# Adding the experts' rows to the residual by accumulating DMAs at the ends of two layers of a one-core kernel

## The chip, the cores and the metric

The kernel runs on one core of a Trainium2 chip, as one launch. The metric is the device time of a run in microseconds (us); of several runs the median is taken.

## The reference

Two layers of a hybrid block over 512 tokens of 1024 values and 256 context tokens. What matters here is the second part of each layer, a mixture of experts, and the step behind it:

```python
hl2 = rmsnorm(xl, g_ffn[l]) * (1 + sc2) + sh2
y = hierarchical_moe(...)          # each token: 2 of 32 experts, (silu(x@w1[e]) * (x@w3[e])) @ w2[e], weighted
xl = xl + ga2 * y                  # the residual; in layer 0 the context rows too
...
return rmsnorm(xl, g_final)        # after layer 1
```

The next layer begins with another `rmsnorm` of the residual, so nothing of it can start on a token tile before that tile's sum is complete. All data are float32.

## The kernel before

The residual lies in SBUF as one tile `X` of 128 partitions x `nt` token tiles x 1024 values, with `nt` = 6 in layer 0 (four token tiles and two of context) and 4 in layer 1. It is filled before the experts start and not touched while they run.

The experts run in the order `seq`, one after another. Their weights come from HBM as six 1 MB pieces each (`eparts`), through a ring of SBUF buffers (`wcycle`, counted by `wcount`), issued by SP in the order of use. An expert gathers its rows (`gather`, an indirect DMA from POOL), multiplies by w1 and w3 (`first`), goes through the activation (`mid`, `hidden`), multiplies by w2 (`second`) and weighs its rows (`out`). The rows of 30 of the 32 experts are then scattered by an indirect DMA from POOL (`send`, line 1528) into a DRAM tensor `yd[l]`, which has two places, `c` = 0 and 1, for each token. The last two experts share a `Group` whose rows stay in SBUF as a high and a low part (`split`); they reach the tokens as a product with a one-hot matrix.

At the end of a layer the loop takes `nt` more buffers from the ring, and SP reads both places of each token tile back, 1 MB a tile (`backs`, line 2010). These reads stand in SP's queue behind the last expert's weights, and wait for the last `send`. VectorE adds them to `X`, two additions a tile (line 2133). The last expert's `second` has two halves of 512 columns; their PSUM is the two banks of one tile `self.p`, the second half reusing the bank that `first` had filled. `end(hf)` evacuates a half (copy `hc` on ScalarE, sum `hs` on VectorE, weight `wg` on VectorE, then the split `keep`). `combine(n_, hf)` forms, for the n_-th tile of `order`, the product with the one-hot matrix plus `ident` x `X` in PSUM, and ScalarE copies the result to `X` (line 2120). From tile n_ = 2 on its PSUM is the tile `acc` (one buffer, `pacc`) or `po` by turns. When both halves of a tile are there, `inv_rms` squares it on ScalarE and POOL makes the two steps to the inverse root (lines 413 and 414). In layer 1 `final` scales and stores the tile; its factor `gfin` is read by a DMA of 512 KB that SP issues ahead of the last expert's six weight pieces, into a buffer taken outside the ring's turn.

A scheduler orders each engine's instructions by its own estimate of when they are ready, unless edges are drawn: `ordered("V", YORD[l])` draws them on VectorE through the additions and the steps of `end`. `SEQ` is the order of the combines on TensorE, in layer 1

```python
((0, 0), "l", (1, 0), (2, 0), (3, 0), (0, 1), (1, 1), (2, 1), (3, 1), 0, 1, 2, 3)
```

where "l" is the second half's `keep` and a bare number is a `final`.

Of the kernel before, what the change touches and what calls it, by code (L numbers as in the profile page):

```python
# [13 lines left out]
ALU = mybir.AluOpType  # L14
# [4 lines left out]
D = 1024  # L19
# [4 lines left out]
NE = 32  # L24
# [17 lines left out]
def xs(n_):  # L42
# [68 lines left out]
DIAG = (1, 1)  # L111
SCT = (1, 1)
LATE = (2, 2)
YORD = ([("hT",), ("y", 0, 0), ("y", 0, 1), ("y", 1, 0), ("hs", 0), ("wg", 0), ("y", 1, 1), ("keep", 1, 0),
# [3 lines left out]
YLB = (3, 3)  # L118
WPRE = (4, 3)
WPS = ("ss", "sa")  # L120
# [135 lines left out]
def program(tc, a, out, dbg=None):  # L256
# [23 lines left out]
    V, S, G, T = [Chained(e_) for e_ in (nc.vector, nc.scalar, nc.gpsimd, nc.tensor)]  # L280
    Y = nc.sync
# [11 lines left out]
    yd = [dr.tile([2 * n_, D], F32, name=f"yd{l}") for l, n_ in enumerate((NT, NL))]  # L293
# [20 lines left out]
    def pacc():  # L314
        return ps.tile([128, 512], F32, name="acc", bufs=1)
# [33 lines left out]
    def wtile(pool=None, n=6, dt=F32):  # L349
        return (pool or wt).tile([128, 2048], dt, name="w", bufs=n)  # L350
# [65 lines left out]
    mark = {}  # L416
# [18 lines left out]
    ct = lambda c_, x_, y_: x_ if c_ else y_  # L435
# [9 lines left out]
    X = xp_.tile([128, 6, D], F32, name="X")  # L445
# [10 lines left out]
    for l in range(2):  # L456
        last = l == 1
# [524 lines left out]
        def wsplit(hf):  # L982

            if hf:
                raw = dfp.tile([128, 4, NT], F32, name="ks1").rearrange("p g t -> p (g t)").rearrange("p (k f) -> p k f", f=512)
                raws = [raw[:, 0:4], raw[:, 4:6]]
            else:
                raws = [wtile().rearrange("p (k f) -> p k f", f=512) for _ in range(2)]
            for w, k0, n in ((raws[0], 0, 4), (raws[1], 4, 2)):
                Y.dma_start(w[:, 0:n], w_out[:, k0:k0 + n, 512 * hf:512 * hf + 512])  # L990
            yield 1
            u = [wtile(dt=F32R).rearrange("p (k f) -> p k f", f=512) for _ in range(3)]
            for i in range(3):
                w, h, lo_ = raws[i // 2][:, 2 * (i % 2):2 * (i % 2) + 2], u[i // 2][:, 2 * (i % 2):2 * (i % 2) + 2], u[(i + 3) // 2][:, 2 * ((i + 1) % 2):2 * ((i + 1) % 2) + 2]
                split(h, lo_, w, V if i in WSV[l] else G)
                if hf:
                    yield 1
            yield [(u[k // 4][:, k % 4], u[(k + 6) // 4][:, (k + 2) % 4]) for k in range(6)]

        wg = [wsplit(0), wsplit(1)]  # L1000
# [10 lines left out]
        X = xp_.tile([128, nt, D], F32, name="X")  # L1011
# [4 lines left out]
        nw2 = NW2[l] - NWA[l]  # L1016
        wta = P.open(f"wta{l}")
        wcount, held = [0], [None]
        wcycle = [(lambda: wta, NWA[l])] * NWA[l] + [(lambda: wt2, nw2)] * nw2 + [(lambda: wt3, 4)] * 4
# [6 lines left out]
        def eparts(e, eng=Y, tail=False):  # L1026
            for nm in ("w1", "w3", "w2"):
                src = wsource(nm, e)
                n = src.shape[1] // 2
                cut = tail and nm == "w2"  # L1030
                for h in range(2):
                    pl, nb = wcycle[wcount[0] % len(wcycle)]
                    w = wtile(pl() if callable(pl) else pl, nb)
                    wcount[0] += 1
                    held[0] = (Y if wcount[0] > SPIN[l] else eng).dma_start(w.rearrange("p (k f) -> p k f", k=2 * n if cut else n),
                                                               src[:, :, 512 * h:512 * h + 512] if cut else src[:, n * h:n * h + n, :])
                    yield w
# [311 lines left out]
        wt2 = P.open(f"wt2{l}")  # L1349
# [139 lines left out]
        wts = pins  # L1489
# [33 lines left out]
        def column(s):  # L1523
            return idn[:, place(s), :]
# [94 lines left out]
        class Expert:  # L1619
# [79 lines left out]
            def second(self):  # L1699

                hT, w2 = self.hT, self.w2
                if self.tail:
                    for hf in range(2):
                        py = self.p[:, ct(hf, slice(0, 512), slice(512, 1024))]
                        for k in range(0, 4, 2):
                            for g in range(2):
                                o = 64 * hf + 32 * g
                                T.matmul(py[o:o + 32, :], hT[:, k + g, 0:32], w2(k + g, hf), start=(k == 0), stop=(k == 2))  # L1708
                            yield 1
                elif self.cap == 32:  # L1710
                    py = self.p[:, 512:1024]
                    for k in range(0, 4, 2):
                        for g in range(4):
                            T.matmul(py[32 * g:32 * g + 32, :], hT[:, k + g // 2, 0:32], w2(k + g // 2, g % 2), start=(k == 0), stop=(k == 2))  # L1714
                        yield 1
                elif self.cap == 64:
                    py = self.p[:, 512:1024]
                    for k in range(4):
                        T.matmul(py[0:64, :], hT[:, k, 0:64], w2(k, 0), start=(k == 0), stop=(k == 3))  # L1719
                        T.matmul(py[64:128, :], hT[:, k, 0:64], w2(k, 1), start=(k == 0), stop=(k == 3))  # L1720
                        yield 1
                else:
                    for hf in range(2):
                        for k in range(4):
                            T.matmul(self.p[:, 512 * hf:512 * hf + 512], hT[:, k, :], w2(k, hf), start=(k == 0), stop=(k == 3))  # L1725
                            yield 1
# [37 lines left out]

            def end(self, hf):

                r, py, g = self.r, self.p[:, ct(hf, slice(0, 512), slice(512, 1024))], self.g
                yl, ys = g.tiles(True)
                sl = slice(512 * hf, 512 * hf + 512)
                h_ = self.hs[32 * hf:32 * hf + 32]  # L1770
                mark["S", "hc", hf] = S.copy(h_, py[64 * hf:64 * hf + 32])
                mark["V", "hs", hf] = V.tensor_tensor(ys[r, sl], py[64 * hf + 32:64 * hf + 64], h_, op=ALU.add)
                mark["V", "wg", hf] = g.weigh(r, hf, sl, ys[r, sl], self.weights())
                yield 1
                g.split(r, hf, yl[64 + r.start:64 + r.stop, sl], 1)
# [58 lines left out]
        def load(n_):  # L1834
            s = seq[n_]
            if s not in wts:
                v = nc.values_load(sid[0:1, s:s + 1], engines=[mybir.EngineType.SP], min_val=0, max_val=NE - 1,
                                   skip_runtime_bounds_check_because=why)
                if last and n_ == NE - 1:
                    gfin.append(wtile(wt2, nw2)[:, 0:D])  # L1840
                    Y.dma_start(gfin[0], a["g_final"].to_broadcast([128, D]))
                wts[s] = list(eparts(v, tail=n_ == NE - 1))

        def gather(n_, idxt, o):
            G.indirect_dma_start(out=o[0:n_, :], out_offset=None, in_=h2d[l][0:nrow, :],  # L1845
# [142 lines left out]
                        pass  # L1988
            ovp.release()

        gfin, es, early, backs = [], [], [], {}
        for n_ in range(NE + 1):
            f = None
            if n_ < NE:
                s = seq[n_]
# [3 lines left out]
                else:  # L1999
                    g = Group(column(s), slots[:, place(s):place(s) + 1] if SCT[l] and n_ < NE - LATE[l] else None)  # L2000
                    small_[0] = g if capacity(l, s) == 32 else None
                f = make(n_, g)
                es.append(f)
                g.apart = APT[l] and n_ >= NE - 2
            if n_ == NE - 1 and SCT[l]:
                for t in ct(last, (0, 1, 2, 3), (4, 5, 0, 1, 2, 3)):
                    pl, nb = wcycle[wcount[0] % len(wcycle)]
                    backs[t] = wtile(pl() if callable(pl) else pl, nb).rearrange("p (c f) -> p c f", c=2)
                    wcount[0] += 1
                    Y.dma_start(backs[t], yd[l].rearrange("(c t p) d -> t p c d", c=2, p=128)[t])  # L2010
            if n_ == NE - 1:
                mark.clear()
                if not last:
# [21 lines left out]
            nb = {32: 2, 64: 4, 128: 8}[e.cap]  # L2035
# [36 lines left out]
            c = run(e.steps, max(0, na - e.done - TUR[l]))  # L2072
# [33 lines left out]
        g = es[-1].g  # L2106
# [23 lines left out]

        for n_, t in enumerate(order) if SCT[l] else ():
            for c_ in range(2):
                mark["V", "y", n_, c_] = V.tensor_add(X[:, t, :], X[:, t, :], backs[t][:, c_])  # L2133
        st = e.second()
        ends = [e.end(0), e.end(1)]
        for _ in range(2):
# [6 lines left out]
        for k_ in SEQ[l]:  # L2143
# [4 lines left out]
            else:  # L2148
                combine(*k_)
                if k_[1]:  # L2150
                    n_, t = k_[0], order[k_[0]]
                    inv_rms(t, X[:, t, :], junk[:, D * (n_ % 2):D * (n_ % 2) + D], ssx[:, t:t + 1], rsx[:, t:t + 1])
        chain(0, "")
        ordered("V", YORD[l])
        wk_.release()
# [29 lines left out]
```

## Time and profile before

| what | value |
|---|---|
| median of 3 runs | 1966.62 us (1966.5 to 1977.33) |
| the profiled execution, its own time | 1979.29 us |
| its span in the profile | 1977.6 us |
| mean granted TensorE clock in it | 0.926 |
| busy share: PE, DVE, ACT, POOL | 86%, 45%, 30%, 21% |
| moved by DMA, mean over the span | 579.21 MB, 293 GB/s |

The profile is one execution of its own, which took 12.7 us more than the median; 1.7 us of its time lie outside the span. Positions in the trace are us from the start of the span. The end of layer 0 lies at about 1003 to 1057, the end of layer 1 at about 1906 to 1977.

### The profile page before, as it was taken

The numbers are of one execution on the slowest core, as the hardware profiler recorded it, in microseconds if no ns is written. First come the engines' busy times: TensorE is split into PE (matmuls) and PEld (weight loads), VectorE is DVE, ScalarE is ACT, GpSimd is POOL, SyncE is SP. The second block draws the span as 40 slices with busy tenths as digits, with TensorE's granted clock in tenths as the row PEclk, the third lists the DMA queues.
The fourth block names the chain that finished last, engine by engine and source line by source line (L and its number), as shares of the span: only waits on it lengthen the run. The fifth ranks groups of instructions, "written<-read, shape, count | busy, mean of one in ns | idle before, by whom it ended". The sixth has DMA issues, their size and how long they took to land. (4 is left out here: it accounts for less than half of the span.)

```text
span 1977.6 us, 24969 instructions
## 1 busy us (share of the span) xinstructions
PE 1695.0 (86%) x9346; PEld 978.2 (49%) x9346; DVE 889.3 (45%) x1487; ACT 584.0 (30%) x1054; POOL 408.4 (21%) x395
## 2 busy tenths in 40 slices
PE   4999998899598999999868997979969987979774
PEld 3767777676333333333327875757633333323321
DVE  3877453775523212222245788648642122121224
ACT  3664353652111111111116664556311000010012
POOL 1245001443311011111004234024321110010000
PEclk8999999998699999999978998999979889999887
DMA  8547735607799999999992546454579999999995
GB/s 309 183 159 245 272 113 117 174 20 258 275 410 399 411 416 407 417 411 412 415 364 105 171 179 242 148 155 129 223 300 405 403 403 416 416 414 418 420 393 189
DMA packets 137838, 579.21 MB, mean 293 GB/s; under 512 B 18734, under 2 KB 54958, under 8 KB 82928
## 3 DMA queue, kind: packets, MB, share of 16 engines
q1 hardware_dynamic: 126368, 553.35, 73.0%
q0 software_dynamic: 9328, 20.87, 2.9%
q10 hardware_dynamic: 2016, 3.34, 0.5%
q8 instruction: 76, 1.25, 0.3%
q14 instruction: 50, 0.41, 0.1%
HBM read 544.74 MB, written 42.05 MB: 297 GB/s over the span
## 5 line engine op out<-in xcount | busy, mean ns | idle before, releaser
L502 PE MATMUL mm<-hh,w 128*128 128x256 f32 (+1 forms) x960 | 191.8, 344 | 10.0 <-ACT w L438 4.7
L1660 PE MATMUL pss<-w,xT 128*64 128x512 f32 x368 | 168.9, 606 | 7.1 <-DMA w<-in_w_dram 7.1
L1659 PE MATMUL pss<-w,xT 128*64 128x512 f32 x368 | 173.7, 614 | 0.0
L1655 PE MATMUL pss<-w,xT 128*32 128x512 f32 x880 | 137.8, 674 | 37.5 <-DMA w<-in_w_dram 37.5
L502 PEld LDWEIGHTS mm<-hh,w 128*128 128x128 f32 x960 | 150.3, 193 | 39.3 <-issue 6.4
L1677 ACT COPY hs<-pss 128x512 f32<-128x512 f32 x53 | 31.0, 585 | 466.5 <-PE pss L1655 216.2
L1845 POOL DMA_INDIRECT xg<-h2d,idx_t x64 | 66.2, 1034 | 471.4 <-PE mm L1645 438.2
L1665 PE MATMUL pss<-w,xT 128*128 128x512 f32 x352 | 156.0, 597 | 1.5 <-DMA w<-in_w_dram 1.5
L1697 DVE TENSOR_TENSOR hT<-hT,mm 128x128 f32<-128x128 f32 (+1 forms) x53 | 18.2, 344 | 260.6 <-ACT hT L1696 260.4
L1528 POOL DMA_INDIRECT yd<-yl,slots x47 | 44.3, 943 | 383.3 <-DVE yl L1577 205.5
L1665 PEld LDWEIGHTS pss<-w,xT 128*128 128x128 f32 x352 | 65.3, 190 | 90.7 <-issue 85.5
L1655 PEld LDWEIGHTS pss<-w,xT 128*32 128x32 f32 x880 | 32.2, 121 | 137.2 <-issue 72.2
L1719 PE MATMUL pss<-w,hT 128*64 128x512 f32 x184 | 88.9, 620 | 11.1 <-DVE hT L1697 11.1
L1725 PE MATMUL pss<-w,hT 128*128 128x512 f32 x176 | 92.7, 675 | 3.1 <-issue 3.1
L502 PE MATMUL mm<-hl,w 128*128 128x256 f32 (+1 forms) x480 | 92.2, 334 | 0.0
L1720 PE MATMUL pss<-w,hT 128*64 128x512 f32 x184 | 88.8, 620 | 0.0
L356 DVE COPY xT<-mm 128x512 f32<-128x512 f32 (+1 forms) x64 | 36.1, 563 | 107.7 <-PE mm L1645 107.0
L502 PEld LDWEIGHTS mm<-hl,w 128*128 128x128 f32 x480 | 74.8, 188 | 9.9
L1659 PEld LDWEIGHTS pss<-w,xT 128*64 128x64 f32 x368 | 47.8, 140 | 62.0 <-issue 57.7
L1660 PEld LDWEIGHTS pss<-w,xT 128*64 128x64 f32 x368 | 48.6, 139 | 57.2 <-issue 46.9
L1577 DVE TENSOR_TENSOR yl<-pss,yl 64x512 f32<-64x512 f32 (+1 forms) x44 | 29.7, 687 | 100.0 <-PE pss L1725 56.0
L1686 PEld LDWEIGHTS mm<-cst,hs 128*128 128x128 f32 x432 | 50.3, 192 | 44.5 <-ACT hs L1677 44.5
(396 smaller groups left out, 3262.4 us busy)
## 6 DMA issues: line engine op xcount, KB each, us to landing
w<-in_w_dram SPq DMA_DIRECT2D x382, 1024.0 KB
w<-in_w_ada_dram SPq DMA_DIRECT2D x48, 1024.0 KB
w<-in_w_in_dram SPq DMA_DIRECT2D x20, 1024.0 KB
yd<-bm SPq DMA_DIRECT2D x20, 512.0 KB
w<-yd SPq DMA_DIRECT2D x10, 1024.0 KB
ks<-st SPq DMA_DIRECT2D x16, 384.0 KB
w<-in_w_out_dram SPq DMA_DIRECT2D x5, 1024.0 KB
h2d<-hp SPq DMA_DIRECT2D x10, 512.0 KB
```

Source lines behind the costliest of these rows:

```text
L356: eng.tensor_copy(o, i)
L502: i_ = T.matmul(o, x_(k), y_(k), start=(n == 0), stop=(n == 23))
L1528: G.indirect_dma_start(out=yd[l][0:2 * nrow, :], out_offset=bass.IndirectOffsetOnAxis(ap=idxt, axis=0), in_=rows, in_offset=None, bounds_c ...
L1655: T.matmul(ph[32 * g:32 * g + 32, 0:512], xT[:, k + g // 2, 0:32], w(k + g // 2), start=(k == 0), stop=(k == 6))
L1659: T.matmul(ph[0:64, 0:512], xT[:, k, 0:64], w1(k), start=(k == 0), stop=(k == 7))
L1660: T.matmul(ph[64:128, 0:512], xT[:, k, 0:64], w3(k), start=(k == 0), stop=(k == 7))
L1665: T.matmul(ph[:, o:o + 512], xT[:, k, :], w(k), start=(k == 0), stop=(k == 7))
L1686: T.matmul(pt[:, 64 * k:64 * k + 64], hs[:, 128 * k:128 * k + 128], ident[:, 64 * g:64 * g + 64], start=(g == 0), stop=(g == 1))
L1719: T.matmul(py[0:64, :], hT[:, k, 0:64], w2(k, 0), start=(k == 0), stop=(k == 3))
L1720: T.matmul(py[64:128, :], hT[:, k, 0:64], w2(k, 1), start=(k == 0), stop=(k == 3))
L1725: T.matmul(self.p[:, 512 * hf:512 * hf + 512], hT[:, k, :], w2(k, hf), start=(k == 0), stop=(k == 3))
L1845: G.indirect_dma_start(out=o[0:n_, :], out_offset=None, in_=h2d[l][0:nrow, :], in_offset=bass.IndirectOffsetOnAxis(ap=idxt, axis=0), bound ...
```

## The change

The reads back into ring buffers, their `backs` and the additions on VectorE are gone. In their place POOL issues, for each token tile and each of the two places, one accumulating DMA of 512 KB that adds rows of `yd[l]` to `X` in SBUF: twelve in layer 0 and eight in layer 1. The two for one tile have the same destination, so the second waits until the first has landed. The reading of `gfin` goes behind the last expert's weights, into the ring's next buffer. The second half of the last expert's `second` writes a PSUM tile of its own (`acc`), no longer a bank of `self.p`. The order drawn on VectorE loses the additions.

```diff
-YORD = ([("hT",), ("y", 0, 0), ("y", 0, 1), ("y", 1, 0), ("hs", 0), ("wg", 0), ("y", 1, 1), ("keep", 1, 0),
...
+YORD = ([("hT",), ("hs", 0), ("wg", 0), ("hs", 1), ("wg", 1), ("keep", 1, 0), ("keep", 1, 1)],) * 2
...
                     for hf in range(2):
-                        py = self.p[:, ct(hf, slice(0, 512), slice(512, 1024))]
+                        self.ph = [self.p[:, 512:1024], pacc()] if hf == 0 else self.ph
+                        py = self.ph[hf]
...
-                r, py, g = self.r, self.p[:, ct(hf, slice(0, 512), slice(512, 1024))], self.g
+                r, py, g = self.r, self.ph[hf], self.g
...
+                wts[s] = list(eparts(v, tail=n_ == NE - 1))
                 if last and n_ == NE - 1:
-                    gfin.append(wtile(wt2, nw2)[:, 0:D])
+                    pl, nb = wcycle[wcount[0] % len(wcycle)]
+                    wcount[0] += 1
+                    gfin.append(wtile(pl() if callable(pl) else pl, nb)[:, 0:D])
                     Y.dma_start(gfin[0], a["g_final"].to_broadcast([128, D]))
-                wts[s] = list(eparts(v, tail=n_ == NE - 1))
...
-            if n_ == NE - 1 and SCT[l]:
-                for t in ct(last, (0, 1, 2, 3), (4, 5, 0, 1, 2, 3)):
-                    pl, nb = wcycle[wcount[0] % len(wcycle)]
-                    backs[t] = wtile(pl() if callable(pl) else pl, nb).rearrange("p (c f) -> p c f", c=2)
-                    wcount[0] += 1
-                    Y.dma_start(backs[t], yd[l].rearrange("(c t p) d -> t p c d", c=2, p=128)[t])
...
         for n_, t in enumerate(order) if SCT[l] else ():
             for c_ in range(2):
-                mark["V", "y", n_, c_] = V.tensor_add(X[:, t, :], X[:, t, :], backs[t][:, c_])
+                G.dma_start(X[:, t, :], yd[l].rearrange("(c t p) d -> t c p d", c=2, p=128)[t, c_], accum_op=ALU.add)
```

## Rows read from the trace of the kernel before

**Rows 1.** The page: the span, the chain by line, the reads back.

```profile
span 1977.6 us, 24969 instructions
...
DMA w<-in_w_dram 16%; PE pss L1665 1%; DMA w<-yd 1%; PE pss L1725 1%; PE pss L1655 1%; PE pss L1660 1%; PE mm L1686 0%; PE pss L1714 0%; PE pss L1708 0%; ACT w L412 0%; ACT X L2120 0%; DVE X L2133 0%; ACT hs L1677 0%; PE mm L1691 0%; PE mm 
...
w<-yd SPq DMA_DIRECT2D x10, 1024.0 KB
```

**Rows 2.** The chain in order of time, end of layer 1: start, us, piece.

```profile
1923.94 18.97 DMA w<-yd
...
1942.93 1.24 DVE X L2133
...
1945.44 0.69 DVE yl L1772
...
1946.18 3.50 PE pss L1708 x8
...
1965.07 1.06 ACT w L412
```

**Rows 3.** Timeline, end of layer 1: start, us, instruction, idle before and releaser.

```profile
1906.12 0.34 SPq L1841 DMA_DIRECT2D w<-in_g_final_dram  x1
...
1915.68 0.91 POOL L1528 DMA_INDIRECT yd<-yl,slots  x1 [29.47 <-DVE yl L1579]
...
1935.22 0.20 PEld L1655 LDWEIGHTS pss<-w,xT 128*32 128x32 f32 x4 [0.66 <-DMA w<-in_w_dram]
...
1941.23 1.91 PE L1708 MATMUL pss<-w,hT 128*32 128x512 f32 x8 [0.69 <-DVE hT L1697]
...
1946.18 3.47 PE L1708 MATMUL pss<-w,hT 128*32 128x512 f32 x8 [3.05 <-DVE yl L1772]
...
1951.67 0.69 DVE L1772 TENSOR_TENSOR yl<-pss,hs 32x512 f32<-32x512 f32 x1
...
1951.78 0.47 PE L1605 MATMUL pss<-yl,oneh 128*128 128x512 f32 x1 [2.13 <-DVE yl L439]
...
1952.56 1.20 PE L1605 MATMUL acc<-yl,oneh 128*128 128x512 f32 x1
```

**Rows 4.** Timeline, end of layer 0 (PE's line is a helper's).

```profile
1012.02 0.91 POOL L1528 DMA_INDIRECT yd<-yl,slots  x1 [33.94 <-DVE yl L1577]
...
1017.88 3.62 SPq L2010 DMA_DIRECT2D w<-yd  x6
...
1022.66 1.91 PE L272 MATMUL pss<-w,hT 128*32 128x512 f32 x8 [0.69 <-DVE hT L1697]
...
1029.29 3.63 PE L272 MATMUL pss<-w,hT 128*32 128x512 f32 x8 [4.72 <-DVE yl L1772]
...
1035.05 0.76 PE L272 MATMUL pss<-w 128*128 128x512 f32 x1 [2.13 <-DVE w L439]
...
1045.18 0.18 POOL L413 TENSOR_SCALAR ssx<-ssx 128x1 f32<-128x1 f32 x1 [11.66 <-ACT w L412]
...
1045.42 0.10 POOL L554 MEMSET xr<- 128x2 f32 x1
...
1045.86 1.17 POOL L414 TENSOR_TENSOR rsx<-ssx,mhalf 128x1 f32<-128x1 f32 x1
...
1056.87 0.59 ACT L2120 COPY X<-po 128x512 f32<-128x512 f32 x1
```

**Rows 5.** Waits of SP's queue, 960 to 1060: us in total, times, longest.

```profile
SPq L2010 <- DMA yd<-yl,slots: 14.0, 1, 14.0
```

**Rows 6.** The scatter's line 1528: from issue to landing.

```profile
DMA to landing us min/median/max: 5.8/6.8/11.5
```

**Rows 7.** The additions' line 2133: ns min/median/max, first and last start.

```profile
L2133 DVE TENSOR_TENSOR X<-X,w x20: 1158/1224/1226, 1024.8 to 1958.8; 128x1024 f32<-128x1024 f32 x20
```

**Rows 8.** Windows: busy time by engine, granted PE clock, DMA share, GB/s.

```profile
1018.00:1035.00 17.00, 8.28 (x40) 2.79 (x32) 10.64 (x19) 3.70 (x7) 0.52 (x1) 0.79 0.98 388
...
1924.00:1943.00 19.00, 11.84 (x72) 3.94 (x72) 4.71 (x9) 2.67 (x5) 0.00 (x0) 0.91 1.03 412
```

More of the change, by code (lines that the diff above doesn't have):

```diff
@@ L1989, in beyond @@
             ovp.release()
-        gfin, es, early, backs = [], [], [], {}
+        gfin, es, early = [], [], []
         for n_ in range(NE + 1):
```

3 rows, old and new, of the table YORD are left out of this document.

## The prediction

> **What bounds the kernel now.** I read the page first [rows 1]: the chain that ended last is mostly the stream of expert weights, and a small part of it, 1%, is the reading back of `yd`. So the change can only act where a stream has ended: at the two layer ends. I then read both ends in the timeline, with the chain for layer 1.
>
> In layer 1 the chain goes from the reads back (landed at 1942.93) through two additions on VectorE to `hs` at 1945.44, and from there to the second half of the last expert's product at 1946.18 [rows 2]. The reader should see two things. The first half of that product was done at 1941.23 + 1.91 = 1943.14, and TensorE then stood for 3.05 us until the first half's `hs` had ended, though the second half writes another bank; and after that pause the same eight matmuls took 3.47 us in place of 1.91 [rows 3]. In layer 0 the same pause is 4.72 us, and the matmuls take 3.63 against 1.91 [rows 4]. There three additions of 1.22 us stand ahead of `hs`; in all there are twenty [rows 7].
>
> Where the DMA engines stand differs. In layer 1 they are full (412 GB/s, share 1.03) until the last weights have landed [rows 8]. In layer 0 SP waited 14.0 us for the last scatter [rows 5] before it could issue the six reads at 1017.88 [rows 4]; the weights were already in, and what fills the engines from 1018 to 1035 (388 GB/s) is the reading itself [rows 8].
>
> **The change part by part.** The sum is made on the profiled execution (1979.3 us, 12.7 above the median); its difference is carried to the median of 1966.6.
>
> *The pause of the second half.* With a tile of its own it can follow the first. Layer 1: 3.05 us of pause and 3.47 - 1.91 = 1.56 of slow matmuls, -4.6 [rows 3]. Layer 0: 4.72 + 1.72 = -6.4 [rows 4]. The wait that is added: `combine(2, 0)` uses the same `acc` buffer, so it, and in TensorE's queue all combines behind it, must wait for the second half's `hs`. Before, that `hs` ended at 1952.36 and the combine began at 1952.56 [rows 3]: it moves with the second half, and costs nothing as long as that half is early.
>
> *The additions.* Twelve of 1.22 us in layer 0 and eight in layer 1 leave VectorE [rows 7]. What of them was on the path is the part ahead of `hs`, which is inside the pause above, and one ahead of the second `keep` in layer 1, 1.2, counted in that layer's sum below. The rest lay beside TensorE's and ScalarE's combines: nothing, as long as the sums now come in time.
>
> *The factor `gfin`.* 512 KB less ahead of the last weights: at 412 GB/s [rows 8] -1.3 in layer 1. Behind the weights it is needed only at the very end, and hidden.
>
> *The accumulating DMAs.* No row shows one. A read back of 1 MB is 2.55 us of all engines at 412 GB/s, so 512 KB is 1.27 [rows 1, 8]. The lower bound is that price, 15.3 us for twelve and 10.2 for eight. An accumulation takes in two operands for each that it writes, the row of `yd` and the row of `X`; if taking in sets the pace, 2.55 us each, 30.6 and 20.4. The far bound is one at a time at the scatter's landing time on the same queue, 5.8 to 11.5 us, median 6.8 [rows 6]. I take 2.55, because the engines are full in the rows nearest to it, so that a second operand has no idle time to go into. By the Trainium skill (Collectives: The Full Stack, the bandwidth ceiling in part 3) a reducing DMA runs at half a copy's rate because it has two source reads on one ring, and not because the addition costs; that too would be 2.55 against 1.27, and no row here shows it.
>
> *Layer 0 with 2.55 each.* The last scatter is in at 1017.88 [rows 4]; SP's queue no longer stands behind it, but POOL's does, with nothing urgent in it before the norm. The first read back was used at 1024.8 [rows 7], 6.9 us after its issue, 4.4 more than its transfer; half of that I put ahead of the bytes, an estimate. With it, and one 1 MB read of the next layer's weights among them, the twelve take from about 1020 to 1053. The two of one tile must follow one another. POOL's order is not the code's: memsets written far behind line 414 stand between 413 and 414 of one tile [rows 4], so I expect first places of several tiles ahead of second places, and the queue kept full. The first tile is then complete at about 1036 to 1038, where TensorE's first combine was at 1035.05; the last at about 1053, and the last copy to `X`, two combines later, at about 1056.5, where it ended at 1057.46 [rows 4]. So of the 6.4 us that the pause gives back, 5.4 go into waiting for `X`: -1.0. With 1.27 each all are in by 1037 to 1039, ahead of their combines, and -6.4 stays.
>
> *Layer 1 with 2.55 each.* The last scatter is issued at 1915.68 [rows 3] and lands at the median 6.8 later [rows 6], about 1922.5; from about 1924.5 the accumulations flow. The last expert's weights are still coming: its fourth piece, the last that `first` needs, was in at 1935.22 [rows 3], without `gfin` at 1933.9. That is 9.4 us of stream still to come, which the accumulations now share. If they go turn about with weights, that piece is 9.4 us late, 1943.3 (bounds: 0 if weights go first, 19 if all eight go ahead; half of each, 4.7, at the plain price). From that piece to the end of the second half it takes 1941.23 - 1935.22 = 6.0 and two halves of 1.9, and the last piece, two further on at 5 us a piece, comes at about 1953.4: the second half ends at about 1955.3, where it ended at 1949.65 [rows 3], +5.6. From there to the last square it took 1966.13 - 1949.65 = 16.5 us [rows 2, 3]. Now the first two of the four first-half combines can be done before, `keep` ends some 3.5 us behind the second half, and ScalarE's four last copies and squares (0.59 + 1.06 each [rows 2, 4], some 0.7 between them) follow: 3.5 + 1.2 + 7.3 = 12.0, -4.5. Together about +1.0. With the plain price the second half ends at about 1948.5 and the layer gains 4.5.
>
> *Sum.* -1.0 + 1.0 = 0: 1966 us. One per cent, 19.7 us, is about what a measurement of this kernel can tell from no change.
>
> **The rivals.**
>
> *As cheap as a plain read.* -6.4 and -4.5 give -11, 1956 us. For it: the addition happens as the bytes pass, and taking in `X` and writing it may overlap. Against it: the engines at 412 GB/s with nothing left.
>
> *One landing after another (slower).* If POOL's order keeps the code's, the second place of each tile holds POOL until the first has landed, and the next tile's first goes with it: seven landings for six tiles, five for four. At the median 6.8 [rows 6] plus 1.27 for the second operand, 8.1 us each, the last tile is in at 1017.9 + 57 = 1075 in layer 0, 22 us behind the 1053 at which its combine wants it, and in layer 1 at 1922.5 + 40 = 1963, some 4 us behind. With the norm's lines 413 and 414 behind them on POOL, +25: 1992 us. The point from which it decides is a landing of about 5 us (7 x 5 = 35 = 1053 - 1018); below it nothing is lost. A price of four plain reads for each accumulation, with the queue full, would give the same: 12 x 5.1 = 61 us in layer 0. For it: scatters of the same queue took 5.8 at best. Against it: the reordering seen on POOL.
>
> *The pause stays.* If the second half waits for something else (the buffer `acc`, or its weights), the two pauses are not given back. In layer 0 that changes little, since `X` is waited for; in layer 1 +4.6, 1971 us.
>
> **How the numbers follow.** The forecast has 0.47, the cheap rival 0.28, the slow one 0.20, the pause that stays 0.05. The range from 1953 (the cheap case, and 2 to 3 us for a faster clock without the pauses) to 1990 (nearly the slow case at 8.1 us) leaves out some 0.15. Faster by over 1% would need twice the cheap case: 0.03. The slow rival is beyond 1% only from about 7.7 us a landing: 0.13. The rest, 0.84, is within 1%.
>
> **What would show it.** In the profile after: no wait of the second half (lines 1708) on `hs`, and its matmuls near 1.9 us each half; POOL's software queue with twenty more DMAs, whose packets take twice the time per byte of the weights' (cheap: the same); in layer 0 the first combine at about 1036 and waiting for a DMA (cheap: 1029, with no wait); in layer 1 the fourth weight piece some 8 us later than 1935 (cheap: 3 to 4), and POOL's issues with first places of several tiles in a row (slow: in pairs, each with a wait of 5 us or more). The forecast is wrong if accumulations cost well over 2.55 us, if weights always go ahead of them, or if POOL issues them only behind work of the norm.

## The result, and the profile after

Side by side on one chip the kernel before took 1966.80 us (median of 4 runs, 1966.50 to 1977.33) and the changed one 1996.19 us (4 runs, 1992.25 to 1998.35): a ratio of 1.0125, 95% interval 1.010 to 1.015, so slower by 1.0 to 1.5%. By the ratio that is 24.6 us, by the two medians 29.4. The forecast was 1966 with a range of 1953 to 1990.

To see where the time went I use two distances that leave out the stretch before the first gather, which wanders by 12 us from profile to profile whatever the kernel:

- **A**, end of layer 0: from the last addition that makes `hT` to the next layer's first product with `gh`.
- **B**, end of layer 1: from `hT` of the last expert but one to the end of the span.

| us | A | B |
|---|---|---|
| before, the profile shown first | 90.8 | 53.6 |
| before, a second profile | 89.5 | 55.1 |
| after | 106.4 | 61.0 |

The stretch between the two is 810 to 811 us in all three. So the change lost 15.6 us in layer 0 and 7.4 us in layer 1, 23.0 together; the forecast had -1.0 and +1.0.

The page of after: the span, the software queue, the accumulations as issued (number, size, median us from issue to landing).

```profile
span 1994.1 us, 24972 instructions
...
q0 software_dynamic: 12208, 31.35, 5.7%
...
X<-yd POOLq DMA_DIRECT2D x20, 512.0 KB, 10.0
```

After's DMA queues from 995 to 1060: packets, MB, share of 16 engines' time in the window.

```profile
q0 software_dynamic: 1808, 6.43, 51.6%
q1 hardware_dynamic: 4599, 8.27, 35.0%
```

51.6% of 65 us is 33.5 us of all engines for layer 0's twelve accumulations and one small scatter: 2.8 us for 512 KB, by the packets' times. The predicted price was 2.55.

After's timeline at the end of layer 0: start, us, instruction, idle before and its releaser.

```profile
999.34 50.25 SPq L394 DMA_DIRECT2D w<-in_w_in_dram  x3
...
1011.47 2.82 POOL L2127 DMA_DIRECT2D X<-yd  x3 [5.35 <-DMA yd<-yl,slots]
...
1019.79 0.86 POOL L2127 DMA_DIRECT2D X<-yd  x1 [5.50 <-DMA X<-yd]
1022.75 0.85 POOL L2127 DMA_DIRECT2D X<-yd  x1 [2.10 <-DMA X<-yd]
1025.70 3.51 POOL L2127 DMA_DIRECT2D X<-yd  x4 [2.10 <-DMA X<-yd]
...
1043.39 0.87 POOL L2127 DMA_DIRECT2D X<-yd  x1 [2.09 <-DMA X<-yd]
...
1028.43 2.08 PE L269 MATMUL pss<-X,cst 128*128 128x512 f32 x2 [2.47 <-DMA X<-yd]
1054.96 0.80 PE L269 MATMUL pss<-w 128*128 128x512 f32 x1 [24.46 <-ACT X L2114]
...
1033.63 1.90 ACT L435 CAST w<-w 128x2048 fp32r<-128x2048 f32 x1 [10.09 <-DMA w<-in_w_in_dram]
...
1052.40 1.90 ACT L435 CAST w<-w 128x2048 fp32r<-128x2048 f32 x1 [16.23 <-DMA w<-in_w_in_dram]
1052.59 1.62 ACTq L359 DMA_DIRECT2D adab<-in_b_ada_dram  x2
1054.32 0.58 ACT L2114 COPY X<-pss 128x512 f32<-128x512 f32 x1
```

The same places of before:

```profile
1021.60 11.80 SPq L397 DMA_DIRECT2D w<-in_w_in_dram  x2
...
1033.00 0.52 POOL L488 MEMSET adab<- 128x512 f32 x1 [20.07 <-PE pss L272]
...
1037.56 0.58 ACT L2120 COPY X<-pss 128x512 f32<-128x512 f32 x1 [0.56 <-PE pss L272]
1038.20 0.79 PE L272 MATMUL pss<-w 128*128 128x512 f32 x1 [0.67 <-ACT X L2120]
...
1048.74 1.89 ACT L438 CAST w<-w 128x2048 fp32r<-128x2048 f32 x1
```

Three engines are to be read against each other. POOL issues the accumulations in rounds, as its waits tell: the first places of three tiles, then their second places one by one, with the last of these the first places of the other three tiles (the row of four), then the second places of those. The landings, and the single issues that wait for them, follow each other by about 2.95 us. The last accumulation, issued at 1043.39, landed 8.6 us later, at 1052.0. TensorE begins its first combine at 1028.43, only 2.47 us late for `X`. Then it stands for 24.46 us, and not for a sum: it waits for ScalarE's copy of that first product to `X`. ScalarE has the copy behind two casts of the next layer's `w_in`, which wait 10.09 and 16.23 us for their loads. SP had issued these two at 999.34 and 1005.22, ahead of the accumulations; before, it issued them only behind the reads back, from 1021.60. Before, too, the first seven of ScalarE's twelve copies stood ahead of the first of these casts, and TensorE waited 0.67 us for the first copy.

The windows of after that answer to [rows 8] and the stretch behind it: busy time of PE, PEld, DVE, ACT, POOL; granted clock, DMA share, GB/s.

```profile
1018.00:1035.00 17.00, 5.64 (x19) 1.22 (x11) 3.42 (x5) 3.14 (x4) 5.21 (x6) 0.60 1.06 213
1035.00:1057.00 22.00, 2.04 (x4) 1.18 (x4) 0.96 (x2) 3.75 (x5) 10.62 (x18) 0.50 0.80 171
```

The engines are as full as before (1.06 against 0.98) and move 213 GB/s in place of 388. That is nearly the doubled price in one row.

After's end of layer 1.

```profile
1931.04 2.80 POOL L2127 DMA_DIRECT2D X<-yd  x3 [6.71 <-DMA yd<-yl,slots]
...
1949.69 1.92 PE L1652 MATMUL pss<-w,xT 128*32 128x512 f32 x14 [1.34 <-DMA w<-in_w_dram]
...
1957.87 3.63 PE L1706 MATMUL pss<-w,hT 128*32 128x512 f32 x8 [3.52 <-DMA w<-in_w_dram]
...
1965.24 0.87 POOL L2127 DMA_DIRECT2D X<-yd  x1 [9.99 <-DMA X<-yd]
...
1965.47 3.63 PE L1706 MATMUL acc<-w,hT 128*32 128x512 f32 x8 [3.97 <-DMA w<-in_w_dram]
...
1971.26 1.34 DVE L436 TENSOR_TENSOR yl<-yl 32x512 fp32r<-32x512 f32 x2
...
1972.09 0.47 PE L1602 MATMUL pss<-yl,oneh 128*128 128x512 f32 x1 [2.99 <-DVE yl L436]
...
1984.84 1.06 ACT L409 ACTIVATE w<-X 128x1024 f32<-128x1024 f32 x1
```

The second half no longer waits for `hs` as in [rows 3], but both halves now wait for weights, which share the engines with the accumulations. The weights for the second half came at 1965.47, and no combine was done before, not even of the first half: both `keep` run together at 1971.26. No combine waited for a sum here: the last accumulation landed at 1970.7.

### The profile page after: what moved, and what is told of

It is laid out like the page before. It is cut to its first block, busy times and chain, and to the rows that moved or that the text cites. A ratio compares the mean times of both kernels' runs of the same rounds, so it can differ in the third digit from the quotient of the medians.

```text
span 1994.1 us, 24972 instructions
## 1 busy us (share of the span) xinstructions
PE 1682.8 (84%) x9346; PEld 969.9 (49%) x9346; DVE 862.7 (43%) x1467; ACT 584.7 (29%) x1054; POOL 429.2 (22%) x415
## 4 chain that ended last, share of the span: by engine, by line
DMA 40%; PE 19%; DVE 4%; issue 2%; ACT 2%; POOL 0%; SPq 0%; ACTq 0%; DVEq 0%; POOLq 0%
DMA w<-in_w_dram 37%; PE mm L499 5%; DMA w<-in_w_in_dram 2%; PE pss L1656 2%; PE acc L269 2%; PE pss L269 1%; PE pss L1662 1%; PE pss L1657 1%; PE pss L1717 1%; PE mm L269 1%; DMA g<-ada 1%; DVE tt L783 1%; PE po L269 1%; PE mm L591 0%; PE po L924 0%
## 5 line engine op out<-in xcount | busy, mean ns | idle before, releaser
L1723 PE MATMUL pss<-w,hT 128*128 128x512 f32 x176 | 88.0, 646 | 3.1 <-issue 3.1
L1657 PEld LDWEIGHTS pss<-w,xT 128*64 128x64 f32 x368 | 48.5, 139 | 62.4 <-issue 50.5
L1574 DVE TENSOR_TENSOR yl<-pss,yl 64x512 f32<-64x512 f32 (+1 forms) x44 | 29.6, 687 | 98.9 <-PE pss L1723 54.4
L269 PE MATMUL acc<-w,yh 128*128 128x512 f32 x198 | 69.7, 435 | 2.9 <-DVE tmp L269 2.9
```

What stands on the lines that cost most here:

```text
L269: i_ = f(*a_, **k_)
L1657: T.matmul(ph[64:128, 0:512], xT[:, k, 0:64], w3(k), start=(k == 0), stop=(k == 7))
```

## The experiments

All times are against runs of the kernel before on the same chip. A and B come from each run's profile.

| | ratio to before (95%) | A | B |
|---|---|---|---|
| `accumulate_in_layer_0_only` | 1.0051 (1.0026 to 1.0076) | 107.5 | 51.5 |
| `accumulate_in_layer_1_only` | 1.0030 (1.0012 to 1.0047) | 87.9 | 64.8 |
| `no_accumulation` | 0.9970 (0.9949 to 0.9991) | 87.7 | 50.5 |
| `no_accumulation_again` | 0.9983 (0.9968 to 0.9999) | 87.3 | 50.7 |
| `own_tile_only` | 0.9977 (0.9961 to 0.9992) | 85.9 | 50.2 |
| `scalar_order` | 1.0100 (1.0067 to 1.0134) | 106.2 | 60.9 |
| `scalar_and_pool_order` | 1984.45 us, before 1978.39, one run each | 96.9 | 61.0 |
| `first_keep_ahead` | 2000.74 us, the same run of before | 108.4 | 60.5 |
| `accumulations_behind_weights` | 1987.61 us, the same run of before | 107.8 | 57.6 |
| `queues_repaired_and_held` | 1.0072 (1.0049 to 1.0094) | 98.9 | 59.5 |

**The parts apart.** The first three kernels put the old reading back, its additions and VectorE's old order (`YORD`) into layer 1, layer 0 or both; the own tile and the moved `gfin` stay.

```diff
+ACC = (1, 0)      # (0, 1); (0, 0)
...
-                G.dma_start(X[:, t, :], yd[l]..., accum_op=ALU.add)
+                if ACC[l]:
+                    G.dma_start(X[:, t, :], yd[l]..., accum_op=ALU.add)
+                else:
+                    mark["V", "y", n_, c_] = V.tensor_add(X[:, t, :], X[:, t, :], backs[t][:, c_])
```

> Layer 0 as in the changed kernel; layer 1 reads back and adds on VectorE as before, with the separate PSUM tile and the moved final scale. If the two layers' losses are separate (17 in layer 0, 9 in layer 1), the run takes about 1966.8 + 17 less 3 to 8 us for the pause that is gone in layer 1: 1976 to 1981 us. If the loss is of layer 1 (weights held up by the accumulations), it is near 1960 to 1966 us.

> Layer 0 reads back and adds on VectorE as before (with the separate PSUM tile); layer 1 as in the changed kernel. Separate losses: 1966.8 + 9 less 0 to 6 us for the pause that is gone in layer 0, 1970 to 1976 us. If the whole loss is of layer 0: 1960 to 1966 us.

> The changed kernel without its accumulating DMAs: both layers read back and add on VectorE as before, with the separate PSUM tile and the final scale behind the weights. Theory (the accumulations are all of the loss, and the pause of the second half was worth its 4 to 6 us in each layer): 1955 to 1961 us. Rival (the pause was covered, the combines wait for the additions anyway): 1964 to 1968 us.

Against before in the same rounds (1972.35 us) the two kernels with one layer each are 12.9 and 6.9 us slower; 9 to 14 and 3 to 9 were expected, so the two losses are separate. The kernel without accumulations, at 1967.07 us, gained 5.3; the ranges expected for it were counted from a before of some 1966.8, so they don't decide. A and B do: the accumulations cost some 20 us of A (106.4 to 108.4 in the runs that have them unrepaired, 85.9 to 87.9 in those without) and 9 to 15 us of B (60.5 to 64.8 against 50.2 to 51.5). The rest of the change gains 2 to 5 us at each end. The kernel without them is thus faster than both kernels of this case, by 0.3% against before.

**Which part gains.** The own tile alone, with `gfin` in its old place, and the kernel without accumulations once more:

> Of the whole change only the second half's own PSUM tile; the final scale keeps its place ahead of the last weights, and rows are read back and added on VectorE as before. If the tile alone gives the 3 us by which the kernel without accumulations shortens layer 0, layer 0 stays at about +88 us from hT to the first gate product (before: +91), and layer 1 ends about 2 us later than in that kernel, because the scale's 512 KB (1.3 us at 412 GB/s) stay ahead of the weights: a time about 1 to 2 us above that kernel, ratio to before 0.998. Rival: the gain comes from the moved scale; then layer 1 here is no shorter than before (+53.6 from hT to the end of the span).

> The kernel without accumulations (own PSUM tile, the final scale moved, reads back and additions on VectorE) a second time, with more rounds: ratio 0.997, interval below 1, if its 3 us in each layer are real; 1.000 if the first comparison was luck of the stretch before the first gather, which spreads over some 13 us.

1968.18 and 1968.44 us against 1972.98. The tile carries the gain, and the moved `gfin` adds none that these runs can tell. In the timeline of `own_tile_only` the halves take turns with no pause, and the first combine follows `hT` (1017.1) by 8.3 us, where it was 12.7 [rows 4]:

```profile
1017.43 1.07 PE L275 MATMUL pss<-w,hT 128*32 128x512 f32 x2 [0.69 <-DVE hT L1700]
1017.46 1.07 PE L275 MATMUL acc<-w,hT 128*32 128x512 f32 x2
...
1025.38 0.77 PE L275 MATMUL pss<-w 128*128 128x512 f32 x1 [4.29 <-DVE w L442]
```

**ScalarE's order in layer 0.** My first theory was that queue alone; the rival, that the sums themselves come late.

```diff
+            ordered("S", [("x", 0, 0), ..., ("x", 3, 0), ("sp", 768), ("x", 3, 1), ("x", 4, 0), ("sp", 1024)])
```

> The changed kernel, with edges on ScalarE alone: the two casts of the next layer's first weight chunks stand behind the copies to X of the tiles, as they do in the kernel before. Theory (ScalarE's queue): in layer 0 the sums of X are in by about 1051, and what costs some 17 us there is that ScalarE waits for those weights ahead of the first copy; the end of layer 0 comes some 15 to 20 us earlier, the run takes 1976 to 1981 us, and the 9 to 12 us that are lost at the end of layer 1 stay. Rival (the sums themselves are late): 1988 us or more, with TensorE's combines waiting for the accumulating DMAs up to the last.

A was 106.2: nothing gained. ScalarE in this run, and POOL:

```profile
1045.06 1.62 ACTq L359 DMA_DIRECT2D adab<-in_b_ada_dram  x2
1046.78 0.59 ACT L2116 COPY X<-pss 128x512 f32<-128x512 f32 x1 [21.18 <-DMA adab<-in_b_ada_dram]
```

```profile
1043.21 0.87 POOL L2129 DMA_DIRECT2D X<-yd  x1 [2.10 <-DMA X<-yd]
...
1044.37 0.66 POOL L485 MEMSET adab<- 128x512 f32 x1
```

Behind the first blocked queue stood a second. ScalarE issues the load of `adab` ahead of its copies, that load wants POOL's memset of `adab`, and POOL has it behind the last accumulation. So the memset went to VectorE as well:

```diff
-            G.memset(adab[0], 0.0)
+            V.memset(adab[0], 0.0)
```

> As the run with ScalarE's casts behind the copies, and the clearing of the small tile adab at the start of layer 1 moved from POOL to VectorE, so that ScalarE's issue of the load into adab, which stands ahead of its first copy to X, no longer waits for a memset behind the last accumulation on POOL. Theory (two in-order queues): ScalarE's first copy to X starts as soon as its combine is done, about 14 us behind the last expert's hT in place of 31, the last copy ends at about 40 in place of 54, set by the landing of the last sums at about 35. Rival (the sums are late): the first copy at 30 or later all the same. From hT to the first gate product of layer 1 about 92 to 97 us in place of 106, if nothing else takes over.

A fell to 96.9, by 9.5 us. What is left is a wait for a sum:

```profile
1033.79 0.87 POOL L2129 DMA_DIRECT2D X<-yd  x1 [8.34 <-DMA X<-yd]
1036.77 0.85 POOL L2129 DMA_DIRECT2D X<-yd  x1 [2.12 <-DMA X<-yd]
1040.26 0.87 POOL L2129 DMA_DIRECT2D X<-yd  x1 [2.64 <-DMA X<-yd]
```

```profile
1034.44 0.80 PE L269 MATMUL po<-w 128*128 128x512 f32 x1
1043.82 2.08 PE L269 MATMUL po<-X,cst 128*128 128x512 f32 x2 [8.59 <-DMA X<-yd]
```

By the order of the combines in the code this is the first half of the fourth tile of six, the first combine to use `po`. It waits for the tenth of the twelve accumulations: the one issued at 1033.79 landed 10.0 us later, at 1043.8. The last two, issued at 1036.77 and 1040.26, landed at 1047.6 and 1050.4, and the combines of the two tiles that want them came later still and waited for none. So the order of the sums is that of the tiles; they come late because each takes about 3 us.

**The price.** The same DMAs with no addition, so that the sums are left out. Layer 1 then routes other rows and the run's time (2129.79 us) isn't comparable; layer 0's end is.

```diff
-                G.dma_start(X[:, t, :], yd[l]..., accum_op=ALU.add)
+                G.dma_start(X[:, t, :], yd[l]...)
```

> The changed kernel with the same twenty DMAs from POOL, but plain ones: they overwrite X and the sums are left out. Theory (an accumulation takes the engines about twice as long as a plain DMA, and the weights share them turn about): the twelve of layer 0 follow each other at about 1.3 us in place of 2.95 and are in some 15 to 20 us earlier, the next layer's weight chunk lands about as much earlier, the last expert's fourth weight piece in layer 1 is late by 3 to 4 us in place of 7; layer 0's end is 10 to 15 us shorter and layer 1's 5 to 8. Rival (issue, landing and waiting on POOL set the pace, not the addition): the same pace as in the changed kernel, and no gain.

Its queues from 995 to 1060, then POOL, then ScalarE's second cast:

```profile
q1 hardware_dynamic: 5300, 10.32, 42.5%
q0 software_dynamic: 1808, 6.43, 27.8%
```

```profile
1016.47 0.54 POOL L2127 DMA_DIRECT2D X<-yd  x1 [4.61 <-DMA X<-yd]
1018.08 0.54 POOL L2127 DMA_DIRECT2D X<-yd  x1 [1.06 <-DMA X<-yd]
...
1029.17 1.90 ACT L435 CAST w<-w 128x2048 fp32r<-128x2048 f32 x1 [5.40 <-DMA w<-in_w_in_dram]
```

The same packets and bytes took 27.8% in place of 51.6%, 18.1 us of all engines against 33.5. The last of the twelve landed 21.2 us behind `hT` in place of 35.0. The cast waited until 1029.17, not 1052.40, and A was 88.5 (hT at 1014.47, product at 1102.93), 17.9 us below after where 10 to 15 were expected, though nothing in ScalarE's or POOL's order had been repaired. That is within about 1 us of the kernels without accumulations (87.3 to 87.9 with the moved `gfin`), so at the plain price the queues cost at most about 1 us.

**Layer 1.** Two edits. First the first half's `keep` ahead of the second half's `hs` on VectorE, where the kernel before had it and the order drawn with the change has not:

```diff
-        [("hT",), ("hs", 0), ("wg", 0), ("hs", 1), ("wg", 1), ("keep", 1, 0), ("keep", 1, 1)]
+        [("hT",), ("hs", 0), ("wg", 0), ("keep", 1, 0), ("hs", 1), ("wg", 1), ("keep", 1, 1)]
```

> The changed kernel, but in layer 1 VectorE's order has the split of the first half (keep 0) ahead of the second half's hs. Theory (with the old place the first-half products wait for the whole second half): the first product starts at about 1965 to 1967 in place of 1972, as soon as X is in, and the end comes 3 to 5 us earlier. Rival (acc is held until the second half's hs, so only two combines can go ahead): 1 to 2 us.

B was 60.5 against 61.0: nothing that one run can tell. `keep` was indeed first, and waited all the same:

```profile
1974.71 0.58 ACT L1770 COPY hs<-acc 32x512 f32<-32x512 f32 x1 [6.73 <-PE acc L1707]
1975.32 0.62 ACT L436 CAST yl<-yl 32x512 fp32r<-32x512 f32 x1
```

The cast that the first `keep` needs stands on ScalarE behind the copy of the second half. It did so in the kernel before:

```profile
1949.70 0.58 ACT L1771 COPY hs<-pss 32x512 f32<-32x512 f32 x1 [5.89 <-PE pss L1708]
1950.30 0.62 ACT L438 CAST yl<-yl 32x512 fp32r<-32x512 f32 x1
```

Then the accumulations held until the last weights have landed:

```diff
+                if last:
+                    tc.add_manual_dep(i_.ins, held[0].ins.name, ...Sync...)
```

> The changed kernel, with the accumulating DMAs of layer 1 made to wait until the last expert's weights have landed. Theory (they take the weights' time on the DMA engines): the last weight pieces come as early as without accumulation and the second half ends some 12 us earlier than in the changed kernel, but the eight accumulations then take 8 x 2.95 = 24 us behind it, so that the end comes at the same time or 2 to 8 us later. Rival (the weights were late for another reason): the weights stay late, and the end is some 15 us later.

```profile
1943.43 2.79 POOL L2127 DMA_DIRECT2D X<-yd  x3 [22.32 <-DMA w<-in_w_dram]
...
1967.38 0.56 POOL L411 TENSOR_TENSOR rsx<-ssx,mhalf 128x1 f32<-128x1 f32 x1
...
1972.02 2.08 PE L2113 MATMUL po<-X,cst 128*128 128x512 f32 x2 [5.31 <-DMA X<-yd]
```

The last expert's `hT` comes 16.5 us behind the one before it, as in the kernel before (16.9; after: 21.6), so sharing is what held the weights back. B is 57.6, 3.4 us below after, where the same or 2 to 8 us more was expected; it stays above before because TensorE now waits for the sums. From 1946 to 1958 of this run no other queue moves a byte:

```profile
q0 software_dynamic: 655, 2.42, 104.4%
```

2.42 MB in 12 us is 202 GB/s, about half of the 412 in [rows 8], or 2.6 us for 512 KB. So the doubled price isn't made by the sharing. (The packets' times add up to over 100%, so a price from shares comes out somewhat high.)

**All repairs together**, and the kernel before for a second profile:

> The change with all three repairs at once: ScalarE's two late weight casts behind the copies to X, the memset of the next layer's tile on VectorE, and layer 1's accumulations held until the last weights have landed. By the theory of two queues in layer 0 and shared engines in layer 1: layer 0 as with the two queue repairs (+97 us from hT to the first gate product, 9 below the change), layer 1 as with the hold (+57.6 to the end of the span, 3 below): 1984, ratio to before 1.006 to 1.008, still slower, because the sums themselves come at 2.95 us each. Rival: once nothing queues behind them the accumulations cost nothing; then 1967 or less.

> The kernel before once more, for a second profile: the stages of both layer ends within 2 us of the first profile's (+90.8 us from hT of layer 0 to the first gate product, +53.6 from hT of layer 1 to the end of the span), the stretch before the first gather below its 521 us. Otherwise the differences by stage told so far rest on one odd execution.

1989.12 us against 1972.98, ratio 1.0072, as expected; A 98.9 and B 59.5, 1.9 us above their expectations. The two queue repairs are thus worth 7.5 us of A here, where they gave 9.5 alone, and the hold 1.5 us of B, where it gave 3.4; each of these is one profile. Repaired, the accumulations still cost 11 to 13 us of A and 8 to 9 of B against the kernels without them.

## Why the prediction was wrong

**The price** was right for engines that do nothing else: 2.55 us predicted, 2.6 measured. In layer 0, with loads beside, the landings came 2.95 us apart. The first landed 8.0 us after its issue, where 2.2 of start and 2.55 of transfer were put: two loads of `w_in` were on the way, not one. So the last accumulation was in 35.0 us behind `hT` (1016.95); the predicted 1053 was 30.7 behind that of before (1022.32). The trace agrees with the half rate that the Trainium skill (Collectives: The Full Stack, the bandwidth ceiling in part 3) tells of the reducing step of a collective: 27.8% against 51.6% for the same bytes, a little less than twice, with the scatter in both.

**"One landing after another"**, the slow rival at 1992, came closest in its number by luck. The second places did go singly, each behind a landing, but landings of up to 17.8 us (median 10.0, page) overlapped and followed each other at the pace of the engines, 2.95 us, not at 8.1.

**Layer 0, -1.0 predicted, +15.6 measured.** The step that failed is "SP's queue no longer stands behind it, but POOL's does, with nothing urgent in it before the norm". Both halves of that sentence hid a cost. SP, no longer held by the reads back, issued two `w_in` loads ahead of the accumulations; their last packets came among these, so that the loads landed at 1033.6 and 1052.4, and ScalarE's casts, which the schedule now puts ahead of its copies, waited for them. And POOL's queue held the memset of `adab`, on which ScalarE waits; in the trace of before it stands there, at 1033.00, ahead of the norm. I costed the wait for `X` on TensorE and no queue of ScalarE. These two together are the 9.5 us that `scalar_and_pool_order` gives back, or 7.5 in the run with all repairs.

The second part of the step was "the last copy to `X`, two combines later": in `scalar_and_pool_order` that copy ended 45.0 us behind `hT` instead of the predicted 34.2. The wait that counts is that of the fourth tile, whose sum was complete 30.3 us behind `hT`, and behind it came not two half-tile copies but six, which took 14.7 us. I had asked only when the last sum is there, and not when each combine wants its own. With both repairs A is still 9 to 11 us over the kernels without accumulations, and TensorE stands 8.59 us in this one wait. The own tile gave -4.3 in A in `own_tile_only` and some -2.6 in the two runs of the kernel without accumulations, where -6.4 stood.

**Layer 1, +1.0 predicted, +7.4 measured.** The terms, each counted from `hT` of the last expert but one: the fourth weight piece +19.3 predicted, +16.6 measured; the last piece +29.4 and +32.3, since the pieces behind the fourth came at 8.2 and 7.6 us and not at 5; the end of the second half +31.3 and +36.0, its matmuls taking 3.63 us and not 1.9; from there to the end of the last square 12.0 and 16.8. The fourth piece was even early; what was mis-sized is the weights behind it, for which I took the accumulations to be nearly over (the last was issued at 1965.24). The last term failed in "the first two of the four first-half combines can be done before": the order drawn with the change puts the first half's `keep` behind the second half's `hs`, and `first_keep_ahead` shows that even without that ScalarE's cast stands behind the copy of the second half, as it did before. From the last square to the end it took 8.2 us instead of 11.5, which is 3.3 back: 1.0 + 4.7 + 4.8 - 3.3 = 7.2.

**The cheap rival** is what its condition said: at the plain price A was 88.5, a gain of 1 to 2 us on before, though not the 6.4 that stood there. (Its layer 1 had a slip in the sum: an end at 1948.5 in place of 1949.65 and the -4.5 behind it make -5.6.) `gfin` gained nothing that the runs can tell, where -1.3 stood. The 2 to 3 us in the range for a faster clock were measured by no run. The pause did go, as forecast.

**Left open.** What an issue of both places tile by tile would give back of the 8.59 us wasn't tried: the fourth tile's sum would be the eighth to land and not the tenth, by the pace of 2.95 us some 5.9 us earlier, an estimate. Nor was ScalarE's order repaired in layer 1, and why the end behind the last square was 3.3 us shorter is not known.

## What to carry to other kernels

Moving an addition into the DMA takes it off an engine that had time and puts it, at twice the bytes' price, on the resource that here was full; look first whether the DMA engines have that much idle time. When a wait is taken from one in-order queue, follow what that queue now issues earlier and what each other engine's queue holds behind the new wait, down to memsets and casts of the next stage: here two such queues, one hidden behind the other, cost 7.5 to 9.5 us, up to half of what the accumulations lost in layer 0. When a stage consumes its inputs in an order, ask for each consumer when its own input is there: here the fourth of six sums held up more than the last. Time the parts of a change one by one: its smallest part, a second PSUM tile, was the only one that gained.

## What the runs showed of the hardware

The doubled price stays when nothing else runs (202 GB/s, 2.6 us for 512 KB, against 412 GB/s of plain reading), so it isn't made by contention. POOL also takes longer to issue an accumulating DMA, 0.85 to 0.93 us against 0.54 for the plain one of the same shape.

What is left of a load when accumulations start comes in slowly. From 1018 to 1044 of after the two queues had:

```profile
q0 software_dynamic: 1348, 4.90, 98.1%
q1 hardware_dynamic: 455, 0.46, 6.3%
```

q1, with the rest of the two `w_in` loads, sent 0.46 MB in 26 us, 18 GB/s, in packets of 1.0 KB on average against 3.6; from 1011 to 1016, before the accumulations' bytes flowed, it had sent 1.45 MB. The Trainium skill (DMA: Bandwidth & Descriptors, the paragraph on arbitration) says that an engine takes turns between its queues packet by packet. These counts do not show it: three packets of the one queue left for each of the other, all engines together, and which engines still held a part of a load is not shown.

TensorE's granted clock was 0.60 from 1018 to 1035 of after, when it worked 5.64 of 17 us, and 0.50, the lower of its two levels, from 1035 to 1057, when it worked 2.04 of 22 us.
